# Where the second row of a gate product is summed, and when the low parts of T are formed

## The chip, the cores and the metric

The kernel runs on one core of a Trainium2 chip. A core has TensorE (PE, matrix products into the PSUM banks), VectorE (DVE), ScalarE (ACT), GpSimd (POOL) and SyncE (SP), each with its own instruction queue, worked off in order; semaphores tie them together, and SP and POOL issue the transfers. The metric is the device time of one execution in microseconds (us), the median of several runs.

## The reference

One block of a transformer in float32, on 512 tokens of width 1024: a feed-forward, a token mixer of two kinds of attention, a second feed-forward, a final norm.

```python
def swiglu(x, w_gate, w_up, w_down):
    return (jax.nn.silu(x @ w_gate) * (x @ w_up)) @ w_down

def reference(x, ...):
    for layer in range(DEPTH):                       # DEPTH = 1
        x = x + 0.5 * swiglu(rmsnorm(x, ffn1_norm[layer]), ...)
        x = x + token_mixer(rmsnorm(x, mix_norm[layer]), ...)
        x = x + 0.5 * swiglu(rmsnorm(x, ffn2_norm[layer]), ...)
    return rmsnorm(x, final_norm)
```

The hidden width of a feed-forward is 2816, that is 22 rows of 128. The change touches the two feed-forwards alone.

## The kernel before

**Products in three parts.** Every float32 matrix is split into a high part (a cast to a shorter format, mostly on ACT) and a low part (the rest, a subtraction on DVE), and every product is the sum of three matmuls: high by high, high by low, low by high (`mm3`, lines 123 to 125). The names of the trace follow from this: `w` is the tile with the split weights, line 382 casts a high part of it (`high`), line 386 subtracts for a low part (`low`).

**Seven products in place of eight.** The first rows of a feed-forward are computed plainly. The others go in pairs (j, j+1), and a pair of rows by two halves of the tokens (`left`, `right`, 256 each) is a 2 by 2 block product, done with seven block products after Winograd. A pair has two units: the gate unit `("g", j)` and the up unit `("u", j)`. Each unit runs the seven products of the list `SEVEN`, every one twelve matmuls 256 wide, into four PSUM banks w, x, y, z:

```python
SEVEN = (("a11", "w", "b11"), ("s3", "z", "t3"), ("s2", "x", "t2"), ("a12", "w", "b21"),
         ("s1", "y", "t1"), ("a22", "x", "t4"), ("s4", "y", "b22"))
```

An entry is the weight block, the bank and the activation block. Sums of weight blocks (`s1` to `s4`) are made by accumulating transfers (`s1`, `s3`) or on DVE (`s2`, `s4`: `total`, lines 364 and 366). Between products banks are carried on: ACT copies w to x after `a11` (line 411), x to y after `s2`, and z to SBUF after `s3`; this last copy is the product P7, kept in the left half of the tile `rbc` (in the code `res["bc"]`) for a gate unit and of `sq` for an up unit. Bank y holds, after `s1`, the right half of the second row less P7; DVE adds P7 to it and stores the sum (line 414, `add`). Then `s4` goes on accumulating in bank y, toward the right half of the first row, so its first matmul must come after that add has read the bank. After `a22`, bank x holds the left half of the second row, which is added in the same way.

**What is done with a unit's banks** stands in `pair_step(t, u, o, banks)`, called after each product `o` with the time `t` at which it should be over. For a gate unit: SiLU of the first row from bank w (left, after `a12`) and bank y (right, after `s4`), into the tile `g0`; the second row's sums into the tile `g1`, and SiLU over it with the factor -1, since the sums have the other sign. For an up unit: `g0` and `g1` are multiplied by the up rows.

**What is kept of a pair.** `kept(j, t1, t0, t2)` forms from `g0` and `g1` the blocks that the down products read, again in high and low parts: `b11`, `b2`, and T, whose two halves are `t0` and `t1`: sums of blocks computed in place in `g0` and `g1`. `t0_parts` and `t1_parts` are the casts (trace: `h3`, `h5`, ACT), `t0_rest` and `t1_rest` the low parts (`h4`, `h6`, DVE). `g0` and `g1` are tiles of a pool of two buffers (tag `ptb`), so the next pair's `g0` takes the buffer that `h4` reads, and its `g1` the one that `h6` reads; the first writer must wait for these.

**The order** on PE, DVE, ACT, SP and POOL is written out by hand: an event is put on a list with a planned time and a rank, and a loop takes events by time, then rank, then order of insertion. `put(time, f, ...)` gives rank 0; `at(time, rank, f, ...)` another. Rank 1 and 1.5 are loads, 2 the sums of weights, 2.5 low parts of weights, 3 their casts, 4 the products themselves. The times only order the instructions; `STEP` is the planned length of one product, `PLAIN_STEP` that of a plain product. Sums of weights are made 5 steps ahead of their product, casts 4, low parts 3.

**The stages of a feed-forward**: plain gate and up rows; a first gate unit `("g", n1)` whose up rows are plain (n1 is 6 in the first feed-forward, 4 in the second); three or four pairs; five plain down products (`p`) and the first group of down units (`d`, seven products each as well); four pairs; three plain down products and the second group. In the names of the trace `a` and `b` at the end stand for the first and second feed-forward: `pyga` is bank y of a gate unit of the first, `pxub` bank x of an up unit of the second.

Of the kernel before, what the change touches and what calls it, by code (L numbers as in the profile page):

```python
# [17 lines left out]
AF = mybir.ActivationFunctionType  # L18
# [4 lines left out]
S = 512  # L23
# [31 lines left out]
STEP, PLAIN_STEP = 1410, 4080  # L55
# [9 lines left out]
def tile_macaron(ctx: ExitStack, tc, xs, xT, wf, wgu1, wst1, wd1, wdg1, wqk, wv, wo, wgu2, wst2, wd2,  # L65
                 wdg2, lams, relb, onehot, addc, out):
    nc = tc.nc
    V, A, G, T = nc.vector, nc.scalar, nc.gpsimd, nc.tensor
# [10 lines left out]
    def slot(i, nm, dt=F32):  # L79
        return sl.tile([P, S], dt, tag=f"slot{i}", name=nm)  # L80
# [117 lines left out]
    def ffn(wgu, wst, wd, wdg, n0, n1, norm, early, res, nm, hooks, ended, first=None,  # L198
# [91 lines left out]
        left, right = slice(0, HS), slice(HS, S)  # L290
# [37 lines left out]
        sums, raws, second, made, half, g, hs = {}, {}, {}, {}, [], {}, {}  # L328
# [72 lines left out]
        def at(time, rank, f, *a):  # L401
            count[0] += 1
            heapq.heappush(events, (time, rank, count[0], f, a))

        def put(time, f, *a):
            at(time, 0, f, *a)
# [6 lines left out]
        def add(o, a, b):  # L413
            V.tensor_tensor(o, a, b, op=ALU.add)

        def mul(o, a, b):
            V.tensor_tensor(o, a, b, op=ALU.mult)
# [7 lines left out]
        def product(t):  # L425
# [22 lines left out]
            if o[0] == "a11":  # L448
                put(starts[t + 1], A.copy, banks["x"], banks["w"])
            elif o[0] == "s2":  # L450
                put(starts[t + 1], A.copy, banks["y"], banks["x"])
            elif u[0] == "d":
                down_step(starts[t + 1], u, o[0], banks)
            else:
                pair_step(starts[t + 1], u, o[0], banks)
# [8 lines left out]
        def pair_step(t, u, o, banks):  # L464
            j = u[1]
            pw, px, py, pz = (banks[b] for b in "wxyz")
            p7 = (sq if u[0] == "u" else res["bc"])[:, left]

            def tile(r):

                if r not in g.setdefault(j, {}):
                    g[j][r] = tp.tile([P, S], F32, tag="ptb", name=f"g{r}{nm}{j}")
                return g[j][r]

            def silu(r, c, p):
                A.activation(tile(r)[:, c], p, AF.Silu)

            def second_row(c, p):
                add(tile(1)[:, c], p, p7)

            def times_up(r, c):
                mul(g[j][r][:, c], ups[j + r][:, c], g[j][r][:, c])

            if o == "s3":
                put(t, A.copy, p7, pz)
            elif u[0] == "g":
                if o == "a12":
                    put(t, silu, 0, left, pw)
                    if j == n1:
                        put(t + STEP, times_up, 0, left)  # L490
                elif o == "s1":
                    put(t, second_row, right, py)
                elif o == "a22":
                    put(t, second_row, left, px)
                    put(t + STEP * (j > n1), lambda: A.activation(
                        g[j][1][:], g[j][1][:], AF.Silu, scale=-1.0))
                elif o == "s4":
                    put(t, silu, 0, right, py)
                    if j == n1:
                        put(t, times_up, 1, slice(0, S))  # L500
                        put(t + STEP, times_up, 0, right)
                        kept(j, t, t - 2 * STEP, t + STEP)
            else:
                g0, g1 = g[j][0], g[j][1]
                if o == "a12":
                    put(t, mul, g0[:, left], pw, g0[:, left])
                elif o == "s1":
                    put(t, add, sq[:, right], py, p7)
                elif o == "a22":
                    put(t, add, sq[:, left], px, p7)  # L510
                    put(t, stt, g1[:], sq[:], -1.0, g1[:], ALU.mult)
                elif o == "s4":
                    put(t, mul, g0[:, right], py, g0[:, right])
                    kept(j, t - STEP, t - 3 * STEP, t)

        def kept(j, t1, t0, t2):

            g0, g1 = g[j][0], g[j][1]  # L520

            def cast(o, a):
                A.copy(o, a)

            def rest(o, a, h):
                V.tensor_tensor(o, a, h.bitcast(F32), op=ALU.subtract)

            def parts(t, h, l, a):
                put(t, cast, h, a)
                put(t + STEP, rest, l, a, h)  # L530

            if j < PLAIN:
                for r, t in ((1, t1), (0, t2)):
                    h = ah[j + r] = slot(j + r, f"ah{nm}{j + r}", F32R)
                    l = al[j + r] = slot(JF + j + r, f"al{nm}{j + r}", F32R)
                    parts(t + STEP, h[:], l[:], g[j][r][:])
                return
            places = [lambda n=n, i=i: slot(i, f"h{n}{nm}{j}", F32R)
                      for n, i in enumerate(PAIR_SLOTS[(j - PLAIN) // 2 % 4])]
            t = {}  # L540

            def b11():
                t["b"] = places[0]()
                A.copy(t["b"][:, left], g0[:, left])

            def b2():
                t["h2"] = places[1]()
                A.copy(t["h2"][:], g1[:])

            def b2_rest():  # L550
                t["l2"] = places[2]()
                rest(t["l2"][:], g1[:], t["h2"][:])

            def t0_parts():
                t["h0"] = places[3]()
                A.copy(t["h0"][:], g0[:])

            def t0_rest():
                t["l0"] = places[4]()
                rest(t["l0"][:], g0[:], t["h0"][:])  # L560

            def t1_parts():
                t["h1"] = places[5]()
                A.copy(t["h1"][:], g1[:])

            def t1_rest():
                t["l1"] = places[6]()
                rest(t["l1"][:], g1[:], t["h1"][:])
                b = hs[j] = {"b11": (t["b"][:, left], t["b"][:, right])}
                for n, i, c in (("b21", 2, left), ("b22", 2, right), ("t1", 0, left),  # L570
                                ("t3", 0, right), ("t4", 1, left), ("t2", 1, right)):
                    b[n] = t[f"h{i}"][:, c], t[f"l{i}"][:, c]

            put(t0 + STEP, b11)
            put(t0 + 2 * STEP, lambda: rest(t["b"][:, right], g0[:, left], t["b"][:, left]))
            put(t1 + STEP, b2)
            n = max(t1, t2)
            put(n, less, g0[:, left], g0[:, left], g0[:, right])
            put(n + STEP, b2_rest)
            put(n + STEP, less, g0[:, right], g1[:, right], g0[:, right])  # L580
            put(n + 2 * STEP, t0_parts)
            put(n + 2 * STEP, stt, g1[:, right], g1[:, right], -1.0, g0[:, left], ALU.subtract)
            put(n + 2 * STEP, stt, g1[:, left], g1[:, right], -1.0, g1[:, left], ALU.subtract)
            put(n + 3 * STEP, t0_rest)

            at(n + 3 * STEP, 5, t1_parts)
            put(n + 4 * STEP, t1_rest)

        def down_step(t, u, o, banks):
            _, group, m = u  # L590
# [184 lines left out]
    n1 = {}  # L775
# [61 lines left out]
    at = {}  # L837
# [535 lines left out]
```

## Time and profile before

| | us |
|---|---|
| Time before, median of 3 runs | 961.75 (961.2 to 962.27) |
| Profiled execution, its own time | 961.41 |
| Its span, first to last instruction | 959.6 |
| First feed-forward, roughly | 0 to 360 |
| Mixer | 360 to 610 |
| Second feed-forward and final norm | 610 to 959.6 |

The mean granted TensorE clock is 0.993. Busy time by stage in us, from the view that sums it over windows of the span:

| Window | PE | PE weight load | DVE | ACT | Granted clock | DMA share |
|---|---|---|---|---|---|---|
| 0 to 30 | 28.98 | 24.09 | 18.87 | 17.89 | 1.00 | 0.69 |
| 30 to 90 | 59.52 | 49.54 | 52.37 | 30.51 | 1.00 | 0.50 |
| 360 to 450 | 88.91 | 78.05 | 63.05 | 51.76 | 1.00 | 0.37 |
| 450 to 610 | 157.71 | 140.03 | 93.06 | 93.03 | 0.99 | 0.28 |
| 610 to 660 | 50.00 | 41.22 | 44.55 | 24.49 | 1.00 | 0.54 |
| 945 to 959.6 | 4.52 | 3.41 | 8.94 | 0.70 | 0.63 | 0.41 |

How to read it: a matmul's row has its start and its length; matmuls overlap, so the distance between two starts is what counts for the time, not the length. In the lists of single instructions, `out<-in` are the tiles, without their buffer numbers, and square brackets at the end hold the idle time of that engine in front of the instruction and what ended it. A line number such as L414 may be that of a small helper (`add` is line 414, whoever calls it).

### The profile page before, as it was taken

What the parts mean: (1) busy time and instruction counts of PE and PEld (TensorE: products, weight loads), DVE (VectorE), ACT (ScalarE), POOL (GpSimd) and SP (SyncE); (2) the same over time, 40 slices, a digit from 0 to 9 for tenths busy, and PEclk for the clock granted to TensorE, in tenths of its full rate; (3) what the DMA queues carried; (4) which work ended last, traced back from release to release, by engine and by line L of the source; (5) the groups of instructions that cost most, each with busy time, mean ns of one, the idle gap of its engine ahead of it and who ended that gap; (6) DMA issues with size and microseconds to landing.
All of it is one profiled execution on the core that took longest, in us unless ns stands there. A gap on an engine that the chain in (4) does not pass through costs nothing.

```text
span 959.6 us, 17173 instructions
## 1 busy us (share of the span) xinstructions
PE 937.5 (98%) x6452; PEld 867.9 (90%) x6452; DVE 725.1 (76%) x1490; ACT 535.6 (56%) x1102; POOL 98.4 (10%) x117
## 2 busy tenths in 40 slices
PE   9999999999999999999999999999999999999995
PEld 7789998999999998988989888889999899999995
DVE  7697887677887896669764547697888677787786
ACT  7455664455664665566756555455666345666462
POOL 0011101012102100000000003110120111220100
PEclk9999999999999999999999999999999999999997
DMA  7175646578756732444232204454773757874732
GB/s 250 60 207 142 155 125 174 138 195 202 186 139 174 195 116 77 133 132 116 83 115 84 69 19 132 132 164 99 184 182 88 201 138 186 221 185 119 185 106 88
DMA packets 60388, 136.71 MB, mean 142 GB/s; under 512 B 6848, under 2 KB 9152, under 8 KB 60304
## 3 DMA queue, kind: packets, MB, share of 16 engines
q1 hardware_dynamic: 46304, 110.14, 35.0%
q0 software_dynamic: 14000, 25.47, 17.0%
q8 instruction: 50, 0.82, 0.4%
q14 instruction: 34, 0.28, 0.1%
HBM read 130.30 MB, written 2.14 MB: 138 GB/s over the span
## 4 chain that ended last, share of the span: by engine, by line
PE 80%; DVE 15%; issue 2%; ACT 1%; DVEq 0%; POOL 0%; POOLq 0%
DVE w L386 5%; PE po L1040 2%; PE pua L123 1%; PE pua L124 1%; PE pua L125 1%; PE pwo L123 1%; PE pwo L124 1%; PE pwo L125 1%; PE pv L900 1%; PE pv L898 1%; PE pv L899 1%; PE pt L1027 1%; PE pq L123 1%; PE pq L125 1%; PE pq L124 1%
## 5 line engine op out<-in xcount | busy, mean ns | idle before, releaser
L1006 DVE CUSTOM_DVE_ANT_0 pr<-sc,strip 128x128 f32<-128x128 f32 (+3 forms) x64 | 30.9, 488 | 35.1 <-PE sc L1004 34.6
L1009 ACT ACTIVATE pr<-pr,mx 128x128 f32<-128x128 f32 (+3 forms) x64 | 36.0, 563 | 31.8 <-DVE mx L1006 30.9
L382 ACT CAST w<-s2b 128x512 fp32r<-128x512 f32 x50 | 31.1, 622 | 21.5 <-DVE s2b L364 19.8
L382 ACT CAST w<-s2a 128x512 fp32r<-128x512 f32 x46 | 28.6, 623 | 22.6 <-DVE s2a L364 19.6
L386 DVE TENSOR_TENSOR w<-s2b,w 128x512 fp32r<-128x512 f32 x50 | 34.2, 685 | 7.9 <-ACT w L382 7.9
L1040 PEld LDWEIGHTS po<-v,ptb 128*128 128x128 f32 x240 | 32.7, 191 | 5.3 <-ACT ptb L1030 2.7
L150 POOL TENSOR_TENSOR sq<-sq,sqt 128x512 f32<-128x512 f32 x7 | 10.9, 1562 | 254.7 <-ACT sqt L149 254.7
L386 DVE TENSOR_TENSOR w<-s2a,w 128x512 fp32r<-128x512 f32 x46 | 31.4, 683 | 6.5 <-ACT w L382 6.5
L898 PE MATMUL pv<-w,xh 128*128 128x256 f32 x128 | 36.2, 283 | 0.0
L900 PE MATMUL pv<-w,xh 128*128 128x256 f32 x128 | 36.2, 283 | 0.0
L899 PE MATMUL pv<-w,xl 128*128 128x256 f32 x128 | 36.2, 282 | 0.0
L1040 PE MATMUL po<-v,ptb 128*128 128x64 f32 (+1 forms) x240 | 32.5, 269 | 1.8 <-ACT ptb L1030 1.7
L1030 ACT COPY ptb<-pt 128x128 f32<-128x128 f32 (+3 forms) x48 | 20.1, 425 | 20.2 <-PE pt L1027 19.9
L123 PE MATMUL pq<-xh,w 128*128 128x512 f32 x64 | 26.9, 421 | 0.0
L123 PE MATMUL pwo<-mh,w 128*128 128x512 f32 x64 | 26.0, 407 | 0.0
L124 PE MATMUL pwo<-ml,w 128*128 128x512 f32 x64 | 25.5, 398 | 0.0
L125 PE MATMUL pwo<-mh,w 128*128 128x512 f32 x64 | 25.5, 398 | 0.0
L124 PE MATMUL pq<-xl,w 128*128 128x512 f32 x64 | 25.1, 392 | 0.0
L123 PE MATMUL pk<-xh,w 128*128 128x512 f32 x64 | 25.1, 392 | 0.0
L125 PE MATMUL pq<-xh,w 128*128 128x512 f32 x64 | 25.1, 392 | 0.0
L125 PE MATMUL pk<-xh,w 128*128 128x512 f32 x64 | 25.0, 391 | 0.0
L124 PE MATMUL pk<-xl,w 128*128 128x512 f32 x64 | 25.0, 390 | 0.0
(661 smaller groups left out, 3994.1 us busy)
## 6 DMA issues: line engine op xcount, KB each, us to landing
raw_qk<-wqk_dram SPq DMA_DIRECT2D x16, 512.0 KB, 3.3
raw0bg<-wst_dram SPq DMA_DIRECT2D x9, 512.0 KB, 5.1
raw_gua<-wgu_dram SPq DMA_DIRECT2D x8, 512.0 KB, 3.9
raw0ag<-wst_dram SPq DMA_DIRECT2D x8, 512.0 KB, 4.6
raw0ad<-wdg_dram SPq DMA_DIRECT2D x8, 512.0 KB, 4.7
strip<-bias_rows SPq DMA_DIRECT2D x16, 256.0 KB, 3.6
raw_v<-wv_dram SPq DMA_DIRECT2D x8, 512.0 KB, 3.3
raw_wo<-wo_dram SPq DMA_DIRECT2D x8, 512.0 KB, 3.2
```

What stands on the lines that cost most here:

```text
L123: T.matmul(po, wh, mh, start=first, stop=False, skip_group_check=on)
L124: T.matmul(po, wh, ml, start=False, stop=False, skip_group_check=on)
L125: T.matmul(po, wl, mh, start=False, stop=last, skip_group_check=on)
L382: A.copy(made[t][0], source(t))
L386: V.tensor_tensor(l, source(t), h.bitcast(F32), op=ALU.subtract)
L898: T.matmul(po, xh[k][:, xs], wh[:, o:o + 256], start=k == 0, stop=False)
L899: T.matmul(po, xl[k][:, xs], wh[:, o:o + 256], start=False, stop=False)
L900: T.matmul(po, xh[k][:, xs], wl[:, o:o + 256], start=False, stop=k == KD - 1)
L1006: V.tensor_tensor_reduce(out=pi, in0=ps[:, :w], in1=st["b"][m][:, w - 1::-1], op0=ALU.add, op1=ALU.min, scale=1.0, scalar=3.0e38, accum_ou ...
L1009: A.activation(pi, pi, AF.Exp, scale=-1.0, bias=st["mx"][:, m, i:i + 1], accum_out=st["ls"][:, m, i:i + 1])
L1030: A.copy(ptb[:, :w], pt[:, :w])
L1040: T.matmul(st["po3"][:, i, d0:d0 + dn], st["ptb", m, i][:, k * P:(k + 1) * P], vt[u // 4, k][:, fo + d0:fo + d0 + dn], start=k == 0, stop= ...
```

## The change

The second row's two sums go into the tile `rbc` in place of `g1`: the right half beside P7, the left half over P7. SiLU then reads all of `rbc` and writes `g1`, which is first allocated there. The SiLU of the first row's left half is ordered one step later and behind the casts of that moment, except in the first gate unit. The low parts of T are ordered two steps later (except after the first gate unit), with rank 1 in place of 0, which sets them behind the `put` events of the same time, the second row's adds among them.

```diff
             pw, px, py, pz = (banks[b] for b in "wxyz")
             p7 = (sq if u[0] == "u" else res["bc"])[:, left]
 
-            def tile(r):
+            def silu(r, c, p, scale=1.0):
 
                 if r not in g.setdefault(j, {}):
                     g[j][r] = tp.tile([P, S], F32, tag="ptb", name=f"g{r}{nm}{j}")
-                return g[j][r]
-
-            def silu(r, c, p):
-                A.activation(tile(r)[:, c], p, AF.Silu)
-
-            def second_row(c, p):
-                add(tile(1)[:, c], p, p7)
+                A.activation(g[j][r][:, c], p, AF.Silu, scale=scale)
...
                 if o == "a12":
-                    put(t, silu, 0, left, pw)
                     if j == n1:
+                        put(t, silu, 0, left, pw)
                         put(t + STEP, times_up, 0, left)
+                    else:
+                        at(t + STEP, 2, silu, 0, left, pw)
                 elif o == "s1":
-                    put(t, second_row, right, py)
+                    put(t, add, res["bc"][:, right], py, p7)
                 elif o == "a22":
-                    put(t, second_row, left, px)
-                    put(t + STEP * (j > n1), lambda: A.activation(
-                        g[j][1][:], g[j][1][:], AF.Silu, scale=-1.0))
+                    put(t, add, p7, px, p7)
+                    put(t + STEP * (j > n1), silu, 1, slice(0, S), res["bc"][:], -1.0)
...
-            put(n + 3 * STEP, t0_rest)
 
             at(n + 3 * STEP, 5, t1_parts)
-            put(n + 4 * STEP, t1_rest)
+            late = 2 * STEP * (j > n1)
+            at(n + 3 * STEP + late, 1, t0_rest)
+            at(n + 4 * STEP + late, 1, t1_rest)
```

## The prediction

> **What bounds the kernel now.** I read the page first, then TensorE's list of waits, then the busy time by stage, then the timelines of TensorE (PE), VectorE (DVE) and ScalarE (ACT) around one of the waits. The page:
>
> ```profile
> span 959.6 us, 17173 instructions
> PE 937.5 (98%) x6452; PEld 867.9 (90%) x6452; DVE 725.1 (76%) x1490; ACT 535.6 (56%) x1102; POOL 98.4 (10%) x117
> ```
>
> PE is busy for 937.5 of 959.6 us; its idle time is 22 us, and no change to the other engines can take off more than this plus the slow restarts behind each gap. The list of PE's waits (instruction, what released it, total us, count, longest) has two rows that belong to the edited code:
>
> ```profile
> PE pyga L123 <- DVE g1a L414: 3.9, 6, 1.3
> PE pygb L123 <- DVE g1b L414: 3.1, 6, 0.5
> ```
>
> Twelve times, six in each feed-forward, the first matmul of a gate unit's product s4 waits for the DVE add of line 414 that empties bank y: 7.0 us together. Busy time by stage (first pair: PE; then PEld, DVE, ACT, POOL, granted clock, DMA share, GB/s):
>
> ```profile
> 90.00:360.00 270.00, 266.01 (x2070) 256.80 (x2069) 219.97 (x419) 155.35 (x309) 36.00 (x43) 1.00 0.62 163
> 660.00:945.00 285.00, 281.89 (x2237) 274.82 (x2237) 224.25 (x413) 161.85 (x326) 38.21 (x44) 1.00 0.61 155
> ```
>
> In these two stretches, which hold all the pairs, the granted clock is 1.00, so nothing but the gaps can be won there, and DVE has 18% and 21% of the time free. It is not DVE's throughput that holds PE but the order of its queue. One of the twelve, PE's timeline (start, length, instruction, idle before):
>
> ```profile
> 265.06 0.28 PE L125 MATMUL pyga<-tta,w 128*128 128x256 f32 x1
> ...
> 266.36 0.28 PE L124 MATMUL pxga<-tta,w 128*128 128x256 f32 x1
> 266.48 0.28 PE L125 MATMUL pxga<-tta,w 128*128 128x256 f32 x1
> 267.27 0.39 PE L123 MATMUL pyga<-xh,w 128*128 128x256 f32 x1 [0.52 <-DVE g1a L414]
> 267.50 0.28 PE L124 MATMUL pyga<-xl,w 128*128 128x256 f32 x1
> ```
>
> Matmuls stand 0.12 us apart. After the last one of a22 (266.48) s4 was due at 266.60 and started at 267.27; the first matmul behind the gap takes 0.23 instead of 0.12 to its successor. The loss is 267.50 - 266.48 - 2 x 0.12 = **0.78 us**, the 0.52 of idle time and 0.26 of drain and restart. Meanwhile DVE has no idle time at all:
>
> ```profile
> 263.19 0.69 DVE L386 TENSOR_TENSOR w<-raw1ag,w 128x512 fp32r<-128x512 f32 x1
> 263.79 0.69 DVE L526 TENSOR_TENSOR h4a<-g0a,h3a 128x512 fp32r<-128x512 f32 x1
> 264.39 0.68 DVE L386 TENSOR_TENSOR w<-s2a,w 128x512 fp32r<-128x512 f32 x1
> 265.00 0.68 DVE L526 TENSOR_TENSOR h6a<-g1a,h5a 128x512 fp32r<-128x512 f32 x1
> 265.60 0.68 DVE L364 TENSOR_TENSOR s2a<-s1au,raw0au 128x512 f32<-128x512 f32 x1
> 266.20 0.68 DVE L386 TENSOR_TENSOR w<-raw0au,w 128x512 fp32r<-128x512 f32 x1
> 266.80 0.42 DVE L414 TENSOR_TENSOR g1a<-pyga,rbc_n 128x256 f32<-128x256 f32 x1
> 267.14 0.68 DVE L386 TENSOR_TENSOR w<-s3au,w 128x512 fp32r<-128x512 f32 x1
> 267.74 0.42 DVE L414 TENSOR_TENSOR g1a<-pxga,rbc_n 128x256 f32<-128x256 f32 x1
> 268.07 0.68 DVE L386 TENSOR_TENSOR w<-s2a,w 128x512 fp32r<-128x512 f32 x1
> ...
> 271.34 0.69 DVE L386 TENSOR_TENSOR w<-raw1au,w 128x512 fp32r<-128x512 f32 x1 [0.73 <-ACT w L382]
> ```
>
> Bank y was complete at 265.06 + 0.28 = 265.34, but the add on it came up only at 266.80, behind six 512-wide instructions 0.60 apart. Two of these, h4a and h6a, are the low parts of T of the pair before, which nothing reads until the down products. PE started 267.27 - 266.80 = 0.47 us after the add did.
>
> **The change, part by part.** Counts are equal: no instruction is added or removed on any engine, and the orders of PE, SP and POOL are the same, DMA issues included. What moves is on DVE and ACT.
>
> *Low parts behind the add.* In the usual pair h4a now stands right behind the y add and h6a behind the x add. The slots that they leave are filled from behind: low part of s2a at 263.79, sum at 264.39, low part of raw0au at 265.00, and the y add at 265.60. Its input is there (265.34). Bank y is free for PE at 265.60 + 0.47 = 266.07, and s4 is due at 266.60: 0.53 us to spare, so the whole 0.78 goes. Behind it on DVE: h4a 265.94, s3au 266.54, x add 267.14 (a22 ends at 266.48 + 0.28 = 266.76), h6a 267.48, and the low part of s2a of the up unit at 268.08, where it was before (268.07). From here on DVE is at its old clock time while PE is 0.78 ahead; it makes that up at the next place where it was idle, the 0.73 in front of 271.34. The nearest deadline in between is that low part. It ends at 268.08 + 0.68 = 268.76. A product lasts 266.48 - 265.06 = 1.42 us; the up unit's first follows s4 at 266.60 + 1.42 = 268.02, and s2, its third, starts at 268.02 + 2 x 1.42 = 270.86. So 2.1 us to spare.
>
> *The first row's SiLU behind a cast, and behind h4a.* ACT before:
>
> ```profile
> 263.44 0.62 ACT L564 CAST h5a<-g1a 128x512 fp32r<-128x512 f32 x1
> 264.57 0.39 ACT L476 ACTIVATE g0a<-pwga 128x256 f32<-128x256 f32 x1 [0.51 <-DVE h4a L526]
> 264.85 0.61 ACT L382 CAST w<-s3au 128x512 fp32r<-128x512 f32 x1
> 266.31 0.62 ACT L382 CAST w<-s2a 128x512 fp32r<-128x512 f32 x1 [0.85 <-DVE s2a L364]
> 266.84 0.61 ACT L382 CAST w<-raw0au 128x512 fp32r<-128x512 f32 x1
> 268.24 0.63 ACT L495 ACTIVATE g1a<-g1a 128x512 f32<-128x512 f32 x1 [0.79 <-DVE g1a L414]
> 268.99 0.39 ACT L476 ACTIVATE g0a<-pyga 128x256 f32<-128x256 f32 x1
> 269.27 0.61 ACT L382 CAST w<-s1au 128x512 fp32r<-128x512 f32 x1
> 270.42 0.36 ACT L411 COPY pxua<-pwua 128x256 f32<-128x256 f32 x1 [0.53 <-PE pwua L125]
> ```
>
> The SiLU of the left half (264.57) writes the buffer that h4a reads; before, it waited 0.51 for it, and now it must wait for an h4a that ends at 265.94 + 0.68 = 266.62. It starts at about 266.71 (0.09 after, as in 264.57 against h4a's end 264.48): 2.14 us later. What is queued behind it: s2a at 266.99, raw0au at 267.51, the second row's SiLU, which needs the end of h6a (268.16, it writes that buffer) and so starts at 268.24 as before; the right half's SiLU at 268.77 (s4 now ends 0.78 earlier and no longer holds it), s1au at 269.05, free at 269.58. Next is the copy of bank w to x, due when PE's first up product ends, 270.42 - 0.78 = 269.64. ACT is in time by 0.06 us, because the idle times 0.85, 0.79 and 0.53 in these rows take up the delay. If it were late, the product that reads bank x starts at 270.86 and the copy takes 0.36, so 0.8 us more may be lost before PE feels it. The s3au cast goes ahead of the SiLU, to 263.96. Cost: nothing, by that cover.
>
> *The second row summed in the tile of P7.* The adds write rbc instead of g1, the SiLU reads rbc: same shapes, same memory, so 0.42, 0.42 and 0.63 as in the rows above. The x add gets a wait on the y add, two instructions ahead of it, long over. The next writer of that tile is an ACT copy in the next gate unit, behind the SiLU in ACT's own order. Cost 0.
>
> *The first pair of the first feed-forward* differs, since its predecessor's h4a stays in front and only h6a passes:
>
> ```profile
> 102.27 0.69 DVE L386 TENSOR_TENSOR w<-raw0au,w 128x512 fp32r<-128x512 f32 x1
> 103.29 0.69 DVE L526 TENSOR_TENSOR h6a<-g1a,h5a 128x512 fp32r<-128x512 f32 x1 [0.33 <-ACT h5a L564]
> 104.08 0.42 DVE L414 TENSOR_TENSOR g1a<-pyga,rbc_n 128x256 f32<-128x256 f32 x1
> 104.56 0.39 PE L123 MATMUL pyga<-xh,w 128*128 128x256 f32 x1 [1.33 <-DVE g1a L414]
> ```
>
> s4 was due at 104.56 - 1.33 - 0.28 + 0.12 = 103.07, so the loss is 1.49 + 0.11 = 1.60. The y add moves up to 102.27 + 0.60 = 102.87, PE starts at 103.35: 0.28 + 0.11 = 0.39 is left, 1.21 is won.
>
> The Trainium skill, "VectorE: DVE Perf Modes", section "The DRAIN you can't avoid", says that a Vector instruction does not start until the pipe behind the one before has emptied. This trace disagrees: 0.68 us instructions start 0.60 apart (263.79, 264.39, 265.00). By the rule the four instructions ahead of that add would put it 4 x 0.08 = 0.3 us later and the sum would be 0.3 smaller; I go by the rows.
>
> *The plain products behind each group of pairs.* h4a and h6a go behind the low part of a plain weight and an addition to x. DVE waits for PE there, in this part of the first feed-forward:
>
> ```profile
> DVE x L423 <- PE pda L125: 10.5, 7, 2.5
> ```
>
> Seven waits, 1.5 us each on average, against 0.60 per instruction moved, and PE has no wait at a plain product in the list. Cost 0; with that cover gone it would be 2 x 0.60 at each of four places, 4.8 us.
>
> *Transfers.* DVE's release of the raw tiles comes up to 0.78 us later against PE. The page gives 4.6 us from issue to landing:
>
> ```profile
> raw0ag<-wst_dram SPq DMA_DIRECT2D x8, 512.0 KB, 4.6
> ```
>
> ACT has no wait for a transfer in the rows above, and the loads run a whole unit (7 x 1.42 = 9.9 us) ahead, which leaves about 5 us. Cost 0.
>
> **Sum:** 11 x 0.78 + 1.21 = **9.8 us**. The profiled execution took 961.41 us, its span and 1.8 us around it; it becomes 951.6. The median of the three runs is 0.34 above it, so I predict **952.0**.
>
> **Rivals.** *One slot late:* the low part of raw0au, now directly in front of the y add, also waits for ACT; were the add 0.60 later (266.20), PE would start at 266.67 and lose 0.07 + 0.11 = 0.18 in each of eleven pairs: 2.0 us less gain, 954.0; with two slots the old loss is back. For it: only 0.53 us to spare. Against it: that cast starts before the 263.44 row, over a microsecond early. *Nothing changes:* s4 also needs its weights, the low part of s2a; if that were its true release, the time would stay at 961.8. Against it: that instruction ends at 265.07, 2.2 us before s4 started, and moves up too. *Slower:* ACT's queue. If its idle times did not absorb the delay of the left SiLU (2.14 us), the copy to bank x would come 2.14 late, PE would wait 2.14 - 0.8 = 1.3 at the third up product in place of 0.78 at s4, and eleven pairs would lose 0.5 each: 5.7 us, 967.5. It decides once the copy is over 0.8 + 0.78 = 1.6 us late. For it: ACT gets there with 0.06 us to spare, and two of its instructions get a wait on ACT itself. Against it: the idle times stand in the rows, and such a wait costs at most the overlap of two casts, which are 0.62 long and 0.53 apart (266.31, 266.84): 0.1.
>
> **How the numbers follow.** 0.78 for the forecast, 0.10 for one slot late, 0.04 for nothing, 0.08 for slower. About 0.2%, 1.9 us, is what a measurement can tell from no change here; both gaining cases lie beyond it, so faster 0.88, same 0.04, slower 0.08. Range: from 950.9 (the first pair's rest of 0.39 gone too, and 0.7 for the spread of the runs) to 956.0 (one slot late, and 2.0 of the 4.8 at the plain places). It leaves out the last two cases.
>
> **What would show it.** Right: PE's waits for line 414 shrink from twelve to one of about 0.1 us; PE busy stays near 937 and the span falls to 950; the pairs' y adds start about 0.9 us before the last matmul of a22 (265.60 against 266.48); the left SiLU starts over 2 us later and waits for h4a; DVE's 0.73 in front of raw1au is nearly gone. Wrong: a PE wait for ACT at pxua, pyua or a weight in the up units, a row of line 414 still at 0.2 us or more in the usual pairs, or a granted clock under 1.00 there.

## The result and the profile after

The changed kernel takes 951.55 us (median of 4 runs, 950.2 to 951.87) against 961.48 for the kernel before in the runs beside it: a ratio of 0.9896, 95% interval 0.9879 to 0.9913, so 10 us faster (8.4 to 11.6). Predicted were 952.0 and a gain of 9.8. The profiled execution took 951.87 us; its page and the list of PE's waits (instruction, releaser, total us, count, longest):

```profile
span 950.1 us, 17200 instructions
PE 934.4 (98%) x6452; PEld 866.6 (91%) x6452; DVE 724.2 (76%) x1490; ACT 533.0 (56%) x1102; POOL 98.2 (10%) x117
```

```profile
...
PE pga L123 <- ACT w L114: 0.5, 2, 0.3
PE pyga L123 <- DVE rbc_n L414: 0.2, 1, 0.2
```

The rows of pygb are gone and of pyga one wait of 0.2 us is left; the rows left out ahead of pga belong to the start, the norms, the mixer and the tail. The row of pga is no work of the change: it lies in the first microseconds, where the two kernels are the same, and it is absent in the executions profiled of four of the kernels below. Each engine has as many instructions as before; the 27 more in the first line are of kinds that the page counts on no engine. PE's order is the same in both kernels, so their stages can be laid side by side by the first start of a tile in each (from PE's timelines; us):

| Stage begins with | Before | After | Gained in the stage before it | Predicted |
|---|---|---|---|---|
| first gate unit, pwga | 84.53 | 84.86 | -0.33 | 0 |
| first plain down product, pda | 157.36 | 155.03 | 2.66 (three pairs) | 1.21 + 2 x 0.78 = 2.77 |
| mixer, pq | 353.16 | 348.52 | 2.31 (four pairs, one without a wait) | 3 x 0.78 = 2.34 |
| first gate unit of the second, pwgb | 658.63 | 653.98 | 0.01 | 0 |
| final norm, bcl | 946.45 | 937.12 | 4.68 (eight pairs, two without a wait) | 6 x 0.78 = 4.68 |

All of the gain, 9.65 us, lies in the three stages with pairs; the start gave 0.33 back in this execution. Read from the starts of s4 alone, the loss falls from 11 x 0.78 + 1.60 = 10.18 us to 0.49 in the first pair, that is by 9.69: s4 accounts for all that the stages gained.

The same pair as in the prediction, PE's timeline, then DVE's:

```profile
263.40 0.28 PE L125 MATMUL pxga<-tta,w 128*128 128x256 f32 x1
263.52 0.28 PE L123 MATMUL pyga<-xh,w 128*128 128x256 f32 x1
263.64 0.28 PE L124 MATMUL pyga<-xl,w 128*128 128x256 f32 x1
```

```profile
260.11 0.68 DVE L386 TENSOR_TENSOR w<-raw1ag,w 128x512 fp32r<-128x512 f32 x1
260.71 0.69 DVE L386 TENSOR_TENSOR w<-s2a,w 128x512 fp32r<-128x512 f32 x1
261.31 0.69 DVE L364 TENSOR_TENSOR s2a<-s1au,raw0au 128x512 f32<-128x512 f32 x1
261.92 0.69 DVE L386 TENSOR_TENSOR w<-raw0au,w 128x512 fp32r<-128x512 f32 x1
262.52 0.42 DVE L414 TENSOR_TENSOR rbc_n<-pyga,rbc_n 128x256 f32<-128x256 f32 x1
262.85 0.68 DVE L523 TENSOR_TENSOR h4a<-g0a,h3a 128x512 fp32r<-128x512 f32 x1
263.45 0.68 DVE L386 TENSOR_TENSOR w<-s3au,w 128x512 fp32r<-128x512 f32 x1
264.06 0.42 DVE L414 TENSOR_TENSOR rbc_n<-pxga,rbc_n 128x256 f32<-128x256 f32 x1
264.39 0.68 DVE L523 TENSOR_TENSOR h6a<-g1a,h5a 128x512 fp32r<-128x512 f32 x1
...
267.48 0.69 DVE L386 TENSOR_TENSOR w<-raw1au,w 128x512 fp32r<-128x512 f32 x1
```

The first matmul of s4 (263.52, pyga) stands 0.12 behind the last of a22 (263.40), like any other two. The y add starts at 262.52, 0.88 ahead of that last matmul; h4a is right behind it, h6a behind the x add, and the idle 0.73 in front of raw1au is gone. ACT there:

```profile
260.88 0.62 ACT L382 CAST w<-s3au 128x512 fp32r<-128x512 f32 x1
263.65 0.38 ACT L473 ACTIVATE g0a<-pwga 128x256 f32<-128x256 f32 x1 [2.15 <-DVE h4a L523]
263.93 0.61 ACT L382 CAST w<-s2a 128x512 fp32r<-128x512 f32 x1
264.44 0.62 ACT L382 CAST w<-raw0au 128x512 fp32r<-128x512 f32 x1
265.17 0.63 ACT L473 ACTIVATE g1a<-rbc_n 128x512 f32<-128x512 f32 x1
265.70 0.37 ACT L473 ACTIVATE g0a<-pyga 128x256 f32<-128x256 f32 x1
265.97 0.61 ACT L382 CAST w<-s1au 128x512 fp32r<-128x512 f32 x1
266.56 0.36 ACT L411 COPY pxua<-pwua 128x256 f32<-128x256 f32 x1
```

The left SiLU stands idle for 2.15 us until h4a is done, and the queue behind it closes up, without an idle time, onto the copy of bank w to x at 266.56.

### The profile page after: what moved, and what is told of

Its sections match the earlier page's. It is cut to its first block, busy times and chain, and to the rows that moved or that the text cites. A ratio compares the mean times of both kernels' runs of the same rounds, so it can differ in the third digit from the quotient of the medians.

```text
span 950.1 us, 17200 instructions
## 1 busy us (share of the span) xinstructions
PE 934.4 (98%) x6452; PEld 866.6 (91%) x6452; DVE 724.2 (76%) x1490; ACT 533.0 (56%) x1102; POOL 98.2 (10%) x117
## 3 DMA queue, kind: packets, MB, share of 16 engines
HBM read 130.30 MB, written 2.14 MB: 139 GB/s over the span
## 4 chain that ended last, share of the span: by engine, by line
PE 91%; DVE 5%; ACT 1%; issue 1%; DMA 1%; SPq 0%; DVEq 0%
PE po L1038 2%; PE pwo L123 1%; PE pwo L124 1%; PE pwo L125 1%; PE pua L123 1%; PE pua L124 1%; PE pua L125 1%; PE pv L898 1%; PE pv L896 1%; PE pv L897 1%; PE pt L1025 1%; PE pq L123 1%; PE pq L125 1%; PE pq L124 1%; PE pdb L125 1%; PE pdb L124 1%
```

## The experiments

Six kernels, all built from the changed one; "before" is the kernel before in the same runs.

**The tile of the sum alone.** The low parts of T and the left SiLU go back to their old places:

```diff
+                    put(t, silu, 0, left, pw)
                     if j == n1:
-                        put(t, silu, 0, left, pw)
                         put(t + STEP, times_up, 0, left)
-                    else:
-                        at(t + STEP, 2, silu, 0, left, pw)
...
+            put(n + 3 * STEP, t0_rest)
             at(n + 3 * STEP, 5, t1_parts)
-            late = 2 * STEP * (j > n1)
-            at(n + 3 * STEP + late, 1, t0_rest)
-            at(n + 4 * STEP + late, 1, t1_rest)
+            put(n + 4 * STEP, t1_rest)
```

> The second row is summed in rbc and its SiLU reads rbc, but the low parts of T and the left SiLU stand where they were before. Theory (all of the gain is the place of h4a and h6a in DVE's queue): twelve waits of s4 for the y add stay, 0.52 us each in eleven pairs and 1.3 in one, and the time stays that of before, 961.5 within 1. Rival (it is the tile of the sum that frees the bank sooner, since the add no longer waits for the buffer of g1): the waits go and the time is near 951.5.

Measured: 961.1 us against 961.06, ratio 1.0003 (0.9993 to 1.0012). PE's waits:

```profile
PE pyga L123 <- DVE rbc_n L414: 3.9, 6, 1.3
PE pygb L123 <- DVE rbc_n L414: 3.1, 6, 0.5
```

Count, total and longest are those of before, only the tile that the add writes has another name. Summing in rbc frees nothing by itself. What it is needed for was not tried apart: with the sum in g1, the y add would be the first writer of g1's buffer, which h6a still reads, so h6a could not stand behind it.

**Only h6a behind the adds.** As above, but `t1_rest` stays late:

```diff
+            put(n + 3 * STEP, t0_rest)
             at(n + 3 * STEP, 5, t1_parts)
-            late = 2 * STEP * (j > n1)
-            at(n + 3 * STEP + late, 1, t0_rest)
-            at(n + 4 * STEP + late, 1, t1_rest)
+            at(n + 4 * STEP + 2 * STEP * (j > n1), 1, t1_rest)
```

> As the changed kernel, but of the two low parts only h6a is moved behind the adds; h4a and the left SiLU stand where they were before. Theory (DVE's queue in slots of 0.60 us): the y add comes one slot earlier than before and one later than in the changed kernel, PE starts s4 0.07 us late, plus 0.11 for the restart, 0.18 in each of eleven pairs: 2.0 us above the changed kernel, 953.5 to 954. Rival (s4's wait ends last at something else, ACT or the weights, and the moves only happened to help): either nothing of the gain (961) or all of it (951.5).

Measured: 952.13 us, ratio 0.9912 (0.9897 to 0.9927). On the same chip the next kernel below, which has no wait in the usual pairs, took 950.05 (0.9890, 0.9875 to 0.9905): 2.1 us less. The expected distance is met, while the absolute time is 1.4 under the 953.5 expected. The chip explains little of that, since the kernel before is only 0.4 lower in this series (961.06 against 961.48); the mean granted clock goes with it: one of the four executions had 0.993, as most of the changed kernel's had, and took 953.51 us, the three with 0.996 took 951.47 to 952.23 (last section). The intervals of the two ratios overlap, so the price itself is read from the trace. DVE and PE in the pair:

```profile
263.12 0.41 DVE L414 TENSOR_TENSOR rbc_n<-pyga,rbc_n 128x256 f32<-128x256 f32 x1
```

```profile
263.39 0.28 PE L125 MATMUL pxga<-tta,w 128*128 128x256 f32 x1
263.59 0.39 PE L123 MATMUL pyga<-xh,w 128*128 128x256 f32 x1
263.81 0.28 PE L124 MATMUL pyga<-xl,w 128*128 128x256 f32 x1
```

The add starts one slot later than in the changed kernel, and s4's first matmul 263.59 - 263.12 = 0.47 after it: 0.20 and 0.22 in place of 0.12 and 0.12, a loss of 0.18, as worked out. The reader is to see that these rows have no bracket: a matmul's row is 0.28 long, so a delay under 0.16 leaves no idle time between rows, and the list of waits has nothing for the usual pairs here. In all eleven usual pairs (those that lost 0.78 before) the loss is 0.18 or 0.19, which makes the 2 us; a list of waits alone would have missed them.

**ACT's cover.** The second row's SiLU, whose result is then written again to the same place, is done once or twice more in each of the 15 pairs, in front of the right half's SiLU:

```diff
                     put(t + STEP * (j > n1), silu, 1, slice(0, S), res["bc"][:], -1.0)
+                    for _ in range(1 * (j > n1)):        # 2 in the second kernel
+                        put(t + STEP, silu, 1, slice(0, S), res["bc"][:], -1.0)
```

> The changed kernel with the second row's SiLU done twice in each of the 15 pairs (same input, same output): ACT's queue, which reaches the copy of bank w to x just in time, is 0.63 to 0.7 us longer there. Theory (0.8 us of cover behind the copy before PE feels it): the copy comes 0.6 to 0.7 late, PE does not wait, 951.5 within 1. Rival (there is no cover, ACT's delay goes to PE at once): 12 to 15 times 0.6 us, 959 to 961.

> The same SiLU three times in each of the 15 pairs, ACT's queue 1.3 us longer. Theory: 0.8 of it is covered, PE waits at the third product of the up unit (pxua, pxub) for ACT's copy, 0.25 us of idle time and 0.6 us of loss in each of 12 to 15 pairs, 7 to 9 us: 958.5 to 960.5. Rival (the cover is larger, since ACT's later idle times count too): 951.5; rival (no cover): 1.3 us each, 967 and more.

Measured: once more 950.05 us (ratio 0.9890, 0.9875 to 0.9905), twice more 957.19 (0.9961, 0.9948 to 0.9973). PE's waits in the second:

```profile
PE pxub L123 <- ACT pxub L411: 1.8, 6, 0.3
PE pxua L123 <- ACT pxua L411: 1.5, 5, 0.3
```

and the place in one pair, ACT and then PE:

```profile
267.20 1.96 ACT L473 ACTIVATE g1a<-rbc_n 128x512 f32<-128x512 f32 x3
269.07 0.37 ACT L473 ACTIVATE g0a<-pyga 128x256 f32<-128x256 f32 x1
269.33 0.61 ACT L382 CAST w<-s1au 128x512 fp32r<-128x512 f32 x1
269.84 0.38 ACT L411 COPY pxua<-pwua 128x256 f32<-128x256 f32 x1
```

```profile
269.70 0.27 PE L125 MATMUL pzua<-tta,w 128*128 128x256 f32 x1
270.27 0.38 PE L123 MATMUL pxua<-txa,w 128*128 128x256 f32 x1 [0.30 <-ACT pxua L411]
270.49 0.28 PE L124 MATMUL pxua<-tta,w 128*128 128x256 f32 x1
```

One SiLU more, 0.65 us, costs nothing; the second one reaches PE. The s2 product was due at 269.70 + 0.12 = 269.82 and started at 270.27, 0.43 after ACT's copy, with 0.10 more to its successor: a loss of 0.55. Eleven pairs lose 0.55 to 0.58 each, the eleven waits of the list; the first pair loses 0.38, too little idle time for the list, and the first pair of each later group loses nothing. Together that is 6.6 us of the 7.1 between the two kernels. The same 0.43 behind the copy at 266.56 in the changed kernel gives 266.99, and there the product starts at 267.78:

```profile
267.78 0.28 PE L123 MATMUL pxua<-txa,w 128*128 128x256 f32 x1
```

So the cover is 0.79 us in this pair, where 0.8 was predicted. The loss per pair and the distance were as expected (0.3 idle for 0.25, 7 us at the low end); the absolute 958.5 was missed by 1.3. Again the granted clock goes with it: the two executions with 0.993 and 0.994 took 958.17 and 958.15, the others, all at 0.995, 956.31 to 957.44. There is a cover, and it ends where it was said to.

**The first pair.** The low parts behind the first gate unit one step later as well:

```diff
-            late = 2 * STEP * (j > n1)
+            late = 2 * STEP if j > n1 else STEP
```

> The changed kernel with the low parts behind the first gate unit of the first feed-forward moved one step later as well, so that h4a stands behind the y add there too. Theory: the last wait for the y add (0.2 us of idle time, 0.5 of loss) is gone, PE has no wait left in the pairs, 0.4 to 0.5 us under the changed kernel run beside it, 951.0: too little for the times to tell, so the trace decides. Rival (the 512-wide cast of h5a holds the place): the wait stays and the time is the same.

> The changed kernel again, as it is, beside the run in front of it: 951.5 within 1, one wait of 0.2 us for the y add in the first pair.

Measured in the same series: 950.44 us (ratio 0.9906, 0.9889 to 0.9922) and 951.49 for the changed kernel (0.9914, 0.9900 to 0.9929); the times can't tell them apart. The trace can. (The edit acts in both feed-forwards, but only the first pair of the first had a wait left.) The pair in the changed kernel as first run, DVE and PE, and then with the edit, DVE and PE:

```profile
102.73 0.68 DVE L386 TENSOR_TENSOR w<-raw0au,w 128x512 fp32r<-128x512 f32 x1
103.33 0.41 DVE L414 TENSOR_TENSOR rbc_n<-pyga,rbc_n 128x256 f32<-128x256 f32 x1
```

```profile
103.30 0.28 PE L125 MATMUL pxga<-tta,w 128*128 128x256 f32 x1
103.80 0.39 PE L123 MATMUL pyga<-xh,w 128*128 128x256 f32 x1 [0.23 <-DVE rbc_n L414]
104.03 0.28 PE L124 MATMUL pyga<-xl,w 128*128 128x256 f32 x1
```

```profile
102.30 0.42 DVE L414 TENSOR_TENSOR rbc_n<-pyga,rbc_n 128x256 f32<-128x256 f32 x1
102.64 0.68 DVE L523 TENSOR_TENSOR h4a<-g0a,h3a 128x512 fp32r<-128x512 f32 x1
```

```profile
102.89 0.28 PE L125 MATMUL pxga<-tta,w 128*128 128x256 f32 x1
103.01 0.28 PE L123 MATMUL pyga<-xh,w 128*128 128x256 f32 x1
103.13 0.28 PE L124 MATMUL pyga<-xl,w 128*128 128x256 f32 x1
```

The changed kernel loses 104.03 - 103.30 - 2 x 0.12 = 0.49 us there; with the edit s4 starts 0.12 behind its predecessor. It is the better version by that half microsecond: s4 loses nothing in any pair any more.

## Why the prediction held

**The bound and the sum.** The order of DVE's queue held PE, not DVE's load. The kernel with the sum alone has the old times and the old waits, so the gain belongs to the place of h4a and h6a (with the left SiLU, which waits for h4a and was not moved by itself); the one with h6a alone shows the price of one slot. In the two stages where all pairs with a wait are usual ones the gains are 2.31 and 4.68 us for 2.34 and 4.68 predicted. One sign did not come: PE's busy time was to stay near 937 and fell to 934.4. Of the 9.7 us only 6.8 are idle time in front of s4 (7.0 before, 0.2 after); the rest is what the sum had as drain and restart, 0.26 a pair, and the page counts that as busy. So it had to fall by some 3 us.

**The slots of 0.60.** The y add moved up two slots, as said; DVE's rows in the changed kernel follow 0.60 apart (261.31, 261.92, 262.52). The rule of the Trainium skill that the prediction weighed ("VectorE: DVE Perf Modes", section "The DRAIN you can't avoid") would, as the prediction took it, have put them 0.68 apart, and the rows after disagree with that as those before did. But the prediction left out a sentence of the same section: "A next op that is not held starts earlier". With it the section leaves room for the 0.60, and the rows are no proof against it.

**The first pair.** This is the term that was off in size: 0.39 us was to be left, 0.49 is. The add did move up by the slot of h6a, to 0.60 behind the low part of raw0au, but DVE reached that low part 0.1 later against PE than in the trace of before, and the remaining wait is 0.2 in place of 0.1. The 0.1 arises at the low part of s2a, which starts 0.47 behind the instruction in front of it (100.92 after 100.45) where before it was 0.34 (100.46 after 100.12); what holds it there stays open. So 1.11 us were won in this pair for 1.21 predicted, which is the shortfall of the first group in the table.

**ACT.** "In time by 0.06 us" was right: the copy starts at 266.56 with no idle time in front, and 0.32 behind the start of the last matmul on bank w (266.24), as before (270.42 behind 270.10), so it is PE that it waits for and not ACT's queue. Measured against the last matmul of a22, the SiLU comes 2.16 later than before (0.25 behind it in place of 1.91 ahead) for a predicted 2.14, and the idle times took it up. The rival built on this queue has the right mechanism, and the cover that it reckons with is the measured one, as the two kernels with more SiLU show, but the changed kernel stays on the safe side of it.

**One slot late, nothing changes.** Both are out: no usual pair has a delay, and the release of s4 was the add. The plain products and the transfers cost nothing that shows: the whole list has no wait of PE at either, and since a list can miss short delays, the sums count too, 9.65 by stages and 9.69 at s4. How large their cover is was only argued.

**What the sum left out.** The span fell by 9.5 us, not 9.8: the first pair gave 0.1 less, the start was 0.33 slower, in code that both kernels share, and the tail behind the last row of the table was 0.2 faster. That the medians differ by 9.9 is in part luck, since what the granted clock does is worth more than the 0.1 between forecast and result (last section).

## What to carry to other kernels

When an engine works its queue off in order and the next engine waits for a bank that it releases, what stands in front of that release is part of the critical path even if nobody reads it for a long time; move such work behind the release before making anything faster. A place in a queue is worth its slots: count how many instructions stand ahead, times their distance (not their length), and check the next deadline behind, on the other queues too, since the work moved will hold a buffer longer. And look at distances between starts, not only at the list of waits: a delay shorter than the overlap of two matmuls leaves no idle time in the profile.

## What the runs showed of the hardware

The granted clock drops for some microseconds late in the mixer in some executions and not in others. In the changed kernel PE waits 1.7 us for ACT there, until 543.27; from 544.5 to 547.5 the granted clock is 0.50, and from 548 on it is 1.00 again. PE's row behind that wait, and the busy times and the clock of that stretch (columns as in the two rows further down):

```profile
543.27 1.19 PE L1038 MATMUL po<-v,ptb 128*128 128x64 f32 x8 [1.70 <-ACT ptb L1028]
```

```profile
544.50:547.50 3.00, 3.00 (x9) 2.42 (x9) 1.35 (x4) 0.00 (x0) 0.00 (x0) 0.50 0.22 49
```

The same wait of 1.7 us stands in the executions without a drop. The changed kernel and the kernel with the edit in the first pair, over 535 to 560 us, where the two do the same work (PE, PE weight load, DVE, ACT, POOL, granted clock, DMA share, GB/s):

```profile
535.00:560.00 25.00, 22.72 (x127) 19.34 (x126) 12.47 (x33) 15.51 (x37) 0.00 (x0) 0.93 0.09 30
```

```profile
535.00:560.00 25.00, 22.71 (x141) 19.59 (x140) 13.54 (x36) 15.80 (x38) 0.00 (x0) 1.00 0.07 22
```

A clock of 0.93 over 25 us would be about 1.7 us if every matmul followed it. The time lost is 1.5: from the first matmul of the mixer (pq) to the first gate unit of the second feed-forward (pwgb) it takes 305.5 us in the six profiled executions with the drop and 303.95 in the two without. It is not a matter of the kernel: of the four executions of the changed kernel one had a mean clock of 0.995 and a span of 948.4 us, three had 0.993 and spans of 949.6 to 950.1. In two profiled executions, that of the edit in the first pair and that of h6a alone, there was no drop; in the six others the window shows 0.93, before and after the change alike, so it falls out of the comparison of those two traces. It does not fall out of every comparison of times: in the series of the first pair the kernel before took 959.51 us, with a mean clock of 0.995 or 0.996 in six of seven executions, and the changed kernel 951.49, with 0.993 in all four, so the gain is 8.0 us there. The execution of before with 0.994 took 960.98, 9.5 more than the changed kernel. Why the drop comes in some executions and not in others was not followed up.
